# Two vectors of adaptive norm columns moved: from layer 0's MLP into its second phase and into the next projection

## The chip, the cores and the metric

The kernel runs on one core of a Trainium2 chip. The metric is device microseconds (us) of a launch, the median of several runs. The core has five engines with a queue each: PE (TensorE, matmuls), DVE (VectorE), ACT (ScalarE), POOL (GpSimd) and SP (SyncE, which here issues the DMA transfers). Each engine works off its own queue strictly in order; semaphores order the engines among each other.

## The reference

Two layers over 1024 tokens of width 1024, all in float32: layer 0 with sparse attention (NSA), layer 1 with sliding-window attention (SWA), each followed by a squared-ReLU MLP of width 4096. Every norm is modulated by a shift, a scale and a gate that come from one condition vector c:

```python
cond = jax.nn.silu(c)
for i in range(DEPTH):
    mod = cond @ ada_w[i] + ada_b[i]              # ada_w[i]: 1024 x 6144
    sh1, sc1, g1, sh2, sc2, g2 = jnp.split(mod, 6, axis=-1)
    h = modulate(rms_norm(x, norm_g[i, 0]), sh1, sc1)
    y = nsa_mixer(...) if i % 2 == 0 else swa_sink_mixer(...)
    x = x + (1 + g1)[:, None, :] * rms_norm(y, norm_g[i, 1])
    h = modulate(rms_norm(x, norm_g[i, 2]), sh2, sc2)
    y = squared_relu_mlp(h, mlp_w_up[i], mlp_w_down[i])
    x = x + (1 + g2)[:, None, :] * rms_norm(y, norm_g[i, 3])
```

So there are six vectors of 1024 to a layer, and each needs a matrix of 1024 x 1024 read once.

## The kernel before

**Stages.** In order of time: the NSA projection and attention, its output projection, layer 0's MLP (a first phase, up, 890 to 1228 us, and a second, down, 1228 to 1555), the SWA projection (about 1531 to 1672), SWA attention with its output projection, and layer 1's MLP (up to 2209, down to 2514). Tokens are eight tiles of 128 rows, t = 0 to 7; norm and turning go by halves of four tiles. Float32 products are made of three matmuls on a high and a low part of each operand (mm3, lines 572 to 574). Both MLP phases use Strassen-like sums of blocks: the first prepares sums of weights (ws, wt) on VectorE and GpSimd, and combines the products (u, sx); the second sums weights (wr) on GpSimd and splits them (st) on ScalarE and VectorE.

**A vector of the modulation ("ada").** `ada_steps` makes one vector of `mod`: eight loads of 128 x 1024 (`adaw`, 512 KB, L311, SP's queue), one L321 and seven L323 on VectorE that scale each by eight of the condition's numbers and add up into an accumulator (`ada`). With `single` a load is a step of its own; otherwise the first step issues three loads and each further step one, two steps ahead. Then `ada_cols` makes a column of it: two transposes (L344) and two reductions (L345, `adas`) on VectorE, four small matmuls (L349) on TensorE, and an addition (L350) on VectorE. `ada_pre(l, which)` makes the two vectors A and B (scale and shift) for a norm of layer l, that of the mixer (which = 0) or that of the MLP (which = 1); `ada_gate(l, which)` makes the gate vector behind it. A and B are used by the norm's last step, L496 on ScalarE, between the turning of the tiles on TensorE (L488, from `xr`) and the split in two parts (L498, L499).

**What sets the order.** There is no planner: the program lists steps (closures), and `spread` mixes two lists evenly. The `side` steps of a phase are mixed among its matmuls; `later(f, n)` puts f n steps behind. `chunks` runs the three parts of the SWA projection (the first four column blocks of q, called q0, then KV by tiles, then q1) and mixes each part with the next one's weight loads and with its share of a `side` list: with 16 side steps over 84 steps, six, six and four. `mlp_down` takes its side steps one to a main step and holds their finishes (the columns) until three quarters of its work are done; they then run one to a main step. Raw tiles for ada loads come from three buffers, and where a pool function is given (`self.slot`) from that pool of 40.

**Around the SWA projection.** Each tile of down's output is gated and added to x (L514, L522; x of before is loaded by L1799, and x of after stored by L1804), its root is taken (L450 on VectorE, L451 on GpSimd), and `xr` is scaled by L472. Four tiles are then turned. q's columns go through rope (L635 and L636 on VectorE, L637 and L639 on GpSimd, L638 on ScalarE) and out by DMA (qd); K's through L663, L666 and L667, V's through L689 and L690. Weights are split by L565 on ScalarE and L566 on VectorE. The first scores of SWA attention are L880 on TensorE, which reads qs from DRAM.

Of the kernel before, what the change touches and what calls it, by code (L numbers as in the profile page):

```python
# [30 lines left out]
LEAD_DOWN = 14  # L31
PAIRS0 = 6
TURN = (10, 20)
SIDE2 = 40
AHEAD = 3
DL = 4
DM = 9
# [7 lines left out]
QT = 5  # L45
# [37 lines left out]
def spread(a, b):  # L83

    out, n = [], 0
    for k, f in enumerate(b):
        while n < len(a) and n * len(b) <= k * len(a):
            out.append(a[n])
            n += 1
        out.append(f)  # L90
    return out + a[n:]


class Trunk:
# [924 lines left out]
    def nsa_unit(self, i, j):  # L1019
# [45 lines left out]
        def branch(b, K, c0, L, mask):  # L1065
# [6 lines left out]
            def head(g):  # L1072
                if g == 0:
                    u[b], nl["nm"], nl["l"] = [], m4("nm"), m4("l")
                if g % per == 0:
                    tiles.append(self.slot(name="p"))
                p, nm, l = tiles[-1][:, g % per * L:g % per * L + L], nl["nm"][:, g:g + 1], nl["l"][:, g:g + 1]
                u[b].append(p)
                s = [self.bank() for _ in range(nb)]
                for z in range(nb):  # L1080
                    self.scores(s[z][:, 0:N], u["q"], g, [v[:, c0 + z * w:c0 + z * w + N] for v in K()])

                def least():
                    for z in range(nb):
                        sl = slice(z * w, z * w + w)
                        self.masked(p[:, sl], s[z][:, 0:w], mask()[:, sl], nm, nm if z else 1e28)

                todo.append([least, lambda: self.exps(p, nm, l)])
                run(g)
# [6 lines left out]
            def weighed():  # L1096
                scale(u[b], nl["l"], b)

            return [(CH + L / 512, lambda g=g: head(g)) for g in range(4)] + [(0.0, lambda g=g: run(g)) for g in range(4, 5 + ML)] + [(0.3, weighed)]

        k0 = max(0, i - 4)
# [343 lines left out]
    def mlp_down(self, sd, w_down, side, post, last):  # L1445
# [101 lines left out]
        def go():  # L1547
            loaded, rest, more = 4, last, list(side)
            self.hold = held = []
            for n, steps in enumerate(main):  # L1550
                if n > 3 * n_q and held:
                    self.later(held.pop(0), 0)
                k = -(-len(more) // max(1, SIDE2 - n))
                steps = spread(more[:k], steps)
# [92 lines left out]
    def run(self):  # L1647
        nc, a = self.nc, self.a
# [31 lines left out]
        parts = self.nsa_project(hT, w_in)  # L1680
# [26 lines left out]
        side = self.ada_gate(0, 0) + self.ada_pre(0, 1)  # L1707
# [4 lines left out]
        for l in range(2):  # L1712
# [12 lines left out]
            take, up = self.up_setup(a["mlp_w_up"][l], lambda l=l: self.cols[l, 1])  # L1725
# [84 lines left out]

            if l == 0:
                parts = self.swa_project(hT2, a["swa_w_in"][0])
            side = self.ada_gate(0, 1, True) + self.ada_pre(1, 0, None, True) if l == 0 else self.ada_gate(1, 1, True)
            self.mlp(up, a["mlp_w_down"][l], side, self.ada_gate(1, 0) + self.ada_pre(1, 1) if l == 0 else [], post,
                     parts[0][0] if l == 0 else [])
            if l == 0:
                self.mark("swaproj")
                self.chunks(parts[:-1] + [(parts[-1][0], parts[-1][1][:4 * QT])])
                src = xd
            self.flush()  # L1820

# [27 lines left out]
```

## Time and profile before

| | us |
|---|---|
| median of 3 runs | 2529.06 (2527.83 to 2530.4) |
| profiled execution | 2529.18 |
| its span | 2527.4 |
| PE busy in the span | 2390.7 (95%) |
| DVE busy | 1924.7 (76%) |
| ACT busy | 1403.4 (56%) |
| POOL busy | 1323.6 (52%) |
| mean DMA rate | 173 GB/s |

The clock of TensorE was 0.979 of full speed on the mean. Busy shares are means over stages with different limits, so the views by stage and the waits of TensorE are of more use than the sums. An engine's idle time costs something only where TensorE comes to wait for it.

### The profile page before, as it was taken

How to read it: one execution, taken by the hardware profiler on the slowest of the kernel's cores; microseconds unless marked ns; L12 is line 12 of the kernel's file. 1: busy time of each engine (PE TensorE's matmuls, PEld its weight loads, DVE VectorE, ACT ScalarE, POOL GpSimd, SP SyncE). 2: the span in 40 equal slices, each digit the busy share in tenths (PEclk: the TensorE clock that was granted, in tenths of full speed). 3: DMA queues.
4: the chain of work that ended last, by engine and by line, in shares of the span. 5: the costliest groups of instructions: out<-in, count | busy, mean ns of one | idle time of the engine just before them, and what ended most of it. 6: DMA issues, size and time to landing. Idle time of an engine off the chain costs nothing.

```text
span 2527.4 us, 36711 instructions
## 1 busy us (share of the span) xinstructions
PE 2390.7 (95%) x11974; PEld 1988.7 (79%) x11974; DVE 1924.7 (76%) x3723; ACT 1403.4 (56%) x2959; POOL 1323.6 (52%) x1308
## 2 busy tenths in 40 slices
PE   6889999999999988999899999988999999999997
PEld 4779888888887767777788887867877688888886
DVE  7865579999895487777799768676768766687756
ACT  4532368898983473454435445377876354545433
POOL 4320566565662146555764622577744554694533
PEclk8999999999999999999999999999999999999999
DMA  7367723132226536556888654444323555597654
GB/s 281 100 216 238 249 80 97 39 93 62 78 68 150 141 117 200 188 199 201 316 327 321 239 186 173 142 140 111 84 86 120 183 176 183 193 319 243 224 186 171
DMA packets 239287, 437.14 MB, mean 173 GB/s; under 512 B 19236, under 2 KB 122872, under 8 KB 239096
## 3 DMA queue, kind: packets, MB, share of 16 engines
q1 hardware_dynamic: 210296, 405.44, 47.6%
q0 software_dynamic: 28800, 29.36, 4.9%
q8 instruction: 94, 1.54, 0.3%
q14 instruction: 97, 0.79, 0.1%
HBM read 320.42 MB, written 114.31 MB: 172 GB/s over the span
## 4 chain that ended last, share of the span: by engine, by line
PE 38%; DVE 5%; POOL 4%; issue 3%; DMA 3%; ACT 2%; SPq 0%; POOLq 0%; DVEq 0%; ACTq 0%
PE b L574 12%; PE b L572 12%; PE b L573 12%; POOL sx L1418 1%; DVE ada L323 1%; POOL qv L637 1%; ACT p L888 1%; PE o L925 1%; PE b L880 1%; DMA wr<-in_mlp_w_down_dram 1%; PE b L903 1%; DMA w<-in_mlp_w_up_dram 1%; DVE hl L1254 1%; DVE wt L1343 1%; DMA adaw<-in_ada_w_dram 0%
## 5 line engine op out<-in xcount | busy, mean ns | idle before, releaser
L572 PE MATMUL b<-hh,wt 128*128 128x512 f32 x896 | 355.5, 397 | 15.5 <-ACT wt L1342 15.3
L574 PE MATMUL b<-hh,wt 128*128 128x512 f32 x896 | 350.7, 395 | 8.7 <-DVE wt L1343 8.5
L573 PE MATMUL b<-st,st 128*128 128x512 f32 x896 | 349.8, 391 | 4.6 <-DVE st L1492 4.6
L573 PE MATMUL b<-hl,wt 128*128 128x512 f32 x896 | 352.2, 393 | 0.0
L574 PE MATMUL b<-st,st 128*128 128x512 f32 x896 | 348.9, 390 | 0.0
L572 PE MATMUL b<-st,st 128*128 128x512 f32 x896 | 330.8, 390 | 2.7 <-DVE u L1373 1.6
L888 ACT ACTIVATE p<-p,nm 128x256 f32<-128x256 f32 (+7 forms) x384 | 250.4, 656 | 46.9 <-DVE nm L884 45.5
L1031 POOL TENSOR_SCALAR p<-p,rl,nsam 128x640 f32<-128x640 f32 (+7 forms) x256 | 199.7, 793 | 136.3 <-DVE rl L1029 98.9
L1492 DVE TENSOR_TENSOR st<-wr,st 128x1024 fp32r<-128x1024 f32 (+1 forms) x128 | 189.8, 1482 | 55.8 <-ACT st L1491 36.5
L910 DVE TENSOR_TENSOR pT<-b,pT 128x512 fp32r<-128x512 f32 (+1 forms) x334 | 215.3, 657 | 21.7 <-ACT pT L909 21.3
L1491 ACT ACTIVATE st<-wr 128x1024 fp32r<-128x1024 f32 (+1 forms) x128 | 122.6, 958 | 195.1 <-POOL wr L1477 89.9
L1492 DVE TENSOR_TENSOR st<-sr,st 128x1024 fp32r<-128x1024 f32 (+1 forms) x128 | 200.8, 1569 | 32.6 <-ACT st L1491 30.4
L572 PEld LDWEIGHTS b<-hh,wt 128*128 128x128 f32 x896 | 170.7, 191 | 58.5 <-ACT wt L1342 24.6
L574 PEld LDWEIGHTS b<-hh,wt 128*128 128x128 f32 x896 | 170.2, 190 | 50.7 <-DVE wt L1343 15.2
L909 ACT ACTIVATE pT<-b 128x512 fp32r<-128x512 f32 (+1 forms) x334 | 185.5, 577 | 42.7 <-PE b L903 40.5
L925 PE MATMUL o<-pT,kv 128*128 128x512 f32 x484 | 194.7, 442 | 7.1 <-DVE pT L910 7.0
L573 PEld LDWEIGHTS b<-st,st 128*128 128x128 f32 x896 | 168.6, 188 | 41.5 <-DVE st L1492 6.8
L903 PE MATMUL b<-ident,p 128*128 128x128 f32 x1296 | 195.4, 274 | 4.7 <-POOL p L1629 2.5
L572 PEld LDWEIGHTS b<-st,st 128*128 128x128 f32 x896 | 168.5, 188 | 39.0 <-DVE u L1373 2.4
L1343 DVE TENSOR_TENSOR wt<-ws,wt 128x512 fp32r<-128x512 f32 x128 | 139.4, 1100 | 77.6 <-ACT wt L1342 76.8
L573 PEld LDWEIGHTS b<-hl,wt 128*128 128x128 f32 x896 | 170.4, 190 | 34.9
L574 PEld LDWEIGHTS b<-st,st 128*128 128x128 f32 x896 | 168.6, 188 | 34.7
(277 smaller groups left out, 6039.6 us busy)
## 6 DMA issues: line engine op xcount, KB each, us to landing
adaw<-in_ada_w_dram SPq DMA_DIRECT2D x96, 512.0 KB, 4.8
sr<-s SPq DMA_DIRECT2D x96, 512.0 KB, 4.5
wr<-in_mlp_w_down_dram SPq DMA_DIRECT2D x96, 512.0 KB, 6.6
w<-in_mlp_w_up_dram SPq DMA_DIRECT2D x76, 512.0 KB, 4.7
s<-sx SPq DMA_DIRECT2D x64, 512.0 KB, 4.2
x<-x SPq DMA_DIRECT2D x48, 512.0 KB, 3.2
s<-u SPq DMA_DIRECT2D x64, 256.0 KB, 2.2
we<-in_mlp_w_down_dram SPq DMA_DIRECT2D x64, 256.0 KB, 4.4
```

The costliest lines, as they stand in the source:

```text
L572: mm(out, s[0], m[0], start=first, stop=False)
L573: mm(out, s[0], m[1], start=False, stop=False)
L574: mm(out, s[1], m[0], start=False, stop=last)
L888: self.nc.scalar.activation(p, p, AF.Exp, scale=-1.0, bias=nm, accum_out=l)
L903: nc.tensor.transpose(pt[:, g * P:(g + 1) * P], p[:, cols], self.ident)
L909: nc.scalar.activation(x[:, 0, 0:w], pt[:, 0:w], AF.Copy)
L910: nc.vector.tensor_tensor(x[:, 1, 0:w], pt[:, 0:w], x[:, 0, 0:w].bitcast(F32), op=ALU.subtract)
L925: nc.tensor.matmul(out, s, m[:, z], start=n == 0 and z == 0, stop=n == len(tiles) - 1 and z == 1)
L1031: nc.gpsimd.tensor_scalar(ps[g], ps[g], rl[:, g:g + 1], gate[:, g, b:b + 1], op0=ALU.mult, op1=ALU.mult)
L1343: nc.vector.tensor_tensor(lo, r, hi.bitcast(F32), op=ALU.subtract)
L1491: nc.scalar.activation(hi, r, AF.Copy)
L1492: nc.vector.tensor_tensor(lo, r, hi.bitcast(F32), op=ALU.subtract)
```

## The change

Layer 0's MLP prepared, beside its own gate (0, 1), all that layer 1's mixer and MLP norms need: A and B of (1, 0) in the first phase, the gate (1, 0) and A and B of (1, 1) in the second. After the change the first phase makes only the gate (0, 1) (16 steps in place of 48), the second makes A and B of (1, 0) and then the gate (1, 0) (24 steps as before), and A and B of (1, 1) are a side list of the SWA projection (16 steps), with loads into the pool of 40. SIDE2, which sets how many side steps go to a main step of down, goes from 40 to 46.

```diff
-SIDE2 = 40
+SIDE2 = 46
...
             if l == 0:
                 parts = self.swa_project(hT2, a["swa_w_in"][0])
-            side = self.ada_gate(0, 1, True) + self.ada_pre(1, 0, None, True) if l == 0 else self.ada_gate(1, 1, True)
-            self.mlp(up, a["mlp_w_down"][l], side, self.ada_gate(1, 0) + self.ada_pre(1, 1) if l == 0 else [], post,
+            side = self.ada_gate(0, 1, True) if l == 0 else self.ada_gate(1, 1, True)
+            self.mlp(up, a["mlp_w_down"][l], side, self.ada_pre(1, 0) + self.ada_gate(1, 0) if l == 0 else [], post,
                      parts[0][0] if l == 0 else [])
             if l == 0:
                 self.mark("swaproj")
-                self.chunks(parts[:-1] + [(parts[-1][0], parts[-1][1][:4 * QT])])
+                self.chunks(parts[:-1] + [(parts[-1][0], parts[-1][1][:4 * QT])], self.ada_pre(1, 1, self.slot))
                 src = xd
             self.flush()
```

Three places in the order of instructions. First, VectorE in layer 0's up phase, around the second ada step of the vector (ws and wt are weight sums, u are products). Before:

```order
L1373 TENSOR_TENSOR u_11328<-b_11329,u_10838 128x512
L323 SCALAR_TENSOR_TENSOR ada_11238<-adaw_11535,cond,ada_11238 128x1024
L1373 TENSOR_TENSOR u_10838<-b_11354,u_11328 128x512
L1343 TENSOR_TENSOR wt_11351<-w_11219,wt_11351 128x512
L1373 TENSOR_TENSOR u_11328<-b_11377,u_10838 128x512
L1373 TENSOR_TENSOR u_11328<-b_11377,u_11328 128x512
```

After:

```order
L1343 TENSOR_TENSOR wt_11432<-ws_11430,wt_11432 128x512
L323 SCALAR_TENSOR_TENSOR ada_11318<-adaw_11684,cond,ada_11318 128x1024
L1373 TENSOR_TENSOR u_11443<-b_11444,u_10887 128x512
L1373 TENSOR_TENSOR u_10887<-b_11469,u_11443 128x512
L1343 TENSOR_TENSOR wt_11466<-w_11337,wt_11466 128x512
L1325 TENSOR_TENSOR ws_11483<-w_11455,w_11457 128x512
```

Layer 1's up phase reads, before and after:

```order
L1343 TENSOR_TENSOR wt_20590<-ws_20588,wt_20590 128x512
L323 SCALAR_TENSOR_TENSOR ada_20476<-adaw_20842,cond,ada_20476 128x1024
L1373 TENSOR_TENSOR u_20601<-b_20602,u_20045 128x512
L1373 TENSOR_TENSOR u_20045<-b_20627,u_20601 128x512
L1343 TENSOR_TENSOR wt_20624<-w_20495,wt_20624 128x512
L1325 TENSOR_TENSOR ws_20641<-w_20613,w_20615 128x512
```

The rows of layer 0 after are those of layer 1, line by line.

Second, SP's queue at the end of down, where the tiles 4 to 7 of x are stored (x_4 to x_7 at L1804) and x of tile 7 is loaded (from x_0_7, L1799). Before:

```order
L1804 DMA x_4_10618<-x_15929 128x1024
L1804 DMA x_5_10619<-x_15960 128x1024
L1799 DMA x_16041<-x_0_7_2934 128x1024
L624 DMA rope_16055<-rope_368 128x1024
L547 DMA w_16534<-in_swa_w_in_dram 128x2x512
L1804 DMA x_6_10620<-x_16005 128x1024
L1804 DMA x_7_10621<-x_16041 128x1024
```

After:

```order
L1804 DMA x_4_10618<-x_15850 128x1024
L1804 DMA x_5_10619<-x_15881 128x1024
L311 DMA adaw_15959<-in_ada_w_dram 128x1024
L311 DMA adaw_15961<-in_ada_w_dram 128x1024
L311 DMA adaw_15963<-in_ada_w_dram 128x1024
L1804 DMA x_6_10620<-x_15926 128x1024
L1799 DMA x_15966<-x_0_7_2934 128x1024
L624 DMA rope_15993<-rope_368 128x1024
L547 DMA w_16482<-in_swa_w_in_dram 128x2x512
L1804 DMA x_7_10621<-x_15966 128x1024
```

Three ada loads and the store of tile 6 now stand ahead of the load of tile 7's x.

Third, VectorE in the KV part, from the rope of K in tile 1 on. Before:

```order
L663 TENSOR_TENSOR kn_16526<-b_16501,cos 128x128
L666 TENSOR_TENSOR rope_16527<-b_16501,sin_190 128x2x32 x2
L690 TENSOR_TENSOR V_16491<-b_16461,V_16491 128x2x64
L566 TENSOR_TENSOR wl_16537<-w_16534,wh_16536 128x4x4x64
L690 TENSOR_TENSOR V_16491<-b_16501,V_16491 128x2x64
L663 TENSOR_TENSOR kn_16565<-b_16540,cos 128x128
```

After:

```order
L663 TENSOR_TENSOR kn_16474<-b_16448,cos 128x128
L666 TENSOR_TENSOR rope_16475<-b_16448,sin_190 128x2x32 x2
L344 STREAM_TRANSPOSE adat_16489<-ada_15958 128x512
L690 TENSOR_TENSOR V_16438<-b_16408,V_16438 128x2x64
L344 STREAM_TRANSPOSE adat_16492<-ada_15958 128x512
L345 TENSOR_REDUCE adas_16488<-adat_16489 128x16
L566 TENSOR_TENSOR wl_16485<-w_16482,wh_16484 128x4x4x64
L690 TENSOR_TENSOR V_16438<-b_16448,V_16438 128x2x64
L345 TENSOR_REDUCE adas_16488<-adat_16492 128x16
```

and TensorE at the same place, where tile 1's last matmuls (into b_16448) and tile 2's first (into b_16502) stand:

```order
L573 MATMUL b_16448<-wl_16250,hh_15773 128x256
L574 MATMUL b_16448<-wh_16249,hl_15774 128x256
L349 MATMUL b_16495<-adas_16488,fold 32x8 x4
L572 MATMUL b_16502<-wh_15982,hh_15701 128x256
L573 MATMUL b_16502<-wl_15983,hh_15701 128x256
```

The column chain of A (1, 1) stands between: VectorE has its second reduction behind an L566, and TensorE has the four L349 that read it ahead of tile 2.

## Rows read from the trace of the kernel before

**Rows 1.** The page, part 1: busy time, share and instructions of each engine.

```profile
PE 2390.7 (95%) x11974; PEld 1988.7 (79%) x11974; DVE 1924.7 (76%) x3723; ACT 1403.4 (56%) x2959; POOL 1323.6 (52%) x1308
```

**Rows 2.** The page, part 4: the chain that ended last, its shares by line.

```profile
PE b L574 12%; PE b L572 12%; PE b L573 12%; POOL sx L1418 1%; DVE ada L323 1%; POOL qv L637 1%; ACT p L888 1%; PE o L925 1%; PE b L880 1%; DMA wr<-in_mlp_w_down_dram 1%; PE b L903 1%; DMA w<-in_mlp_w_up_dram 1%; DVE hl L1254 1%; DVE wt L1343 1%; DMA adaw<-in_ada_w_dram 0%
```

**Rows 3.** Busy us by stretch: length, PE, PEld, DVE, ACT, POOL, PEclk, DMA, GB/s.

```profile
945.60:1228.52 282.92, 270.39 (x1174) 217.70 (x1173) 212.66 (x266) 129.10 (x217) 157.36 (x106) 0.98 0.59 202
1936.20:2209.47 273.27, 267.83 (x1170) 217.54 (x1170) 191.01 (x243) 132.58 (x220) 155.13 (x109) 0.99 0.51 178
1228.52:1325.74 97.22, 89.84 (x380) 71.64 (x379) 91.05 (x53) 36.91 (x42) 77.96 (x37) 0.98 0.91 336
2209.47:2294.67 85.20, 85.20 (x377) 70.57 (x376) 66.20 (x33) 36.06 (x42) 76.54 (x38) 1.00 0.90 313
1570.00:1640.00 70.00, 67.54 (x395) 59.02 (x394) 46.33 (x89) 28.30 (x46) 36.74 (x32) 0.98 0.44 139
1640.00:1720.00 80.00, 65.34 (x343) 54.14 (x342) 56.19 (x181) 53.73 (x162) 63.98 (x87) 0.91 0.56 154
```

**Rows 4.** Waits of PE in layer 0's up phase: us, times, longest.

```profile
PE b L574 <- DVE wt L1343: 6.2, 4, 2.9
...
PE b L349 <- DVE adas L345: 1.7, 2, 1.1
```

**Rows 5.** The same in layer 1's up phase.

```profile
PE b L574 <- DVE wt L1343: 0.4, 1, 0.4
```

**Rows 6.** Timeline of PE after the turn: start, us, [idle before, releaser].

```profile
1245.37 0.50 PE L573 MATMUL b<-st,st 128*128 128x512 f32 x1 [2.31 <-DVE st L1492]
```

**Rows 7.** Timeline of POOL at the turns to down, layers 0 and 1.

```profile
1224.12 1.29 POOL L1476 TENSOR_TENSOR wr<-wr,we 128x512 f32<-128x512 f32 x1 [3.17 <-PE b L574]
...
2198.90 1.29 POOL L1476 TENSOR_TENSOR wr<-wr,we 128x512 f32<-128x512 f32 x1 [0.59 <-PE b L574]
```

**Rows 8.** L323 in layer 0's down: duration ns min/median/max, starts.

```profile
L323 DVE SCALAR_TENSOR_TENSOR ada<-adaw,cond,ada x21: 1272/2202/2325, 1237.0 to 1361.9; 128x1024 f32<-128x1024 f32 x21
```

**Rows 9.** Timeline of DVE, a column chain in layer 0's up phase.

```profile
1205.12 1.30 DVE L344 STREAM_TRANSPOSE adat<-ada 128x512 f32<-128x512 f32 x2
...
1208.11 0.68 DVE L345 TENSOR_REDUCE adas<-adat 128x16 f32<-128x512 f32 x1
```

**Rows 10.** Timeline of SP's queue at the end of down.

```profile
1561.52 0.38 SPq L1799 DMA_DIRECT2D x<-x  x1
...
1566.26 2.34 SPq L1804 DMA_DIRECT2D x<-x  x2
```

**Rows 11.** The page, part 6: loads of ada, KB each, us to landing.

```profile
adaw<-in_ada_w_dram SPq DMA_DIRECT2D x96, 512.0 KB, 4.8
```

**Rows 12.** Timeline of PE at the turning of tiles 4 to 7.

```profile
1573.93 0.88 PE L488 MATMUL b<-ident,xr 128*128 128x128 f32 x6 [0.80 <-DVE xr L472]
1576.37 1.32 PE L488 MATMUL b<-ident,xr 128*128 128x128 f32 x8 [1.57 <-ACT h L496]
```

**Rows 13.** Timeline of DVE at the same place.

```profile
1571.44 2.43 DVE L472 TENSOR_SCALAR xr<-x,r 128x1024 f32<-128x1024 f32 x2 [0.56 <-POOL r L451]
```

**Rows 14.** Timeline of DVE in the KV part.

```profile
1607.32 0.29 DVE L663 TENSOR_TENSOR kn<-b,cos 128x128 f32<-128x128 f32 x1 [2.34 <-POOL kn L667]
...
1609.70 2.09 DVE L566 TENSOR_TENSOR wl<-w,wh 128x1024 fp32r<-128x1024 f32 x1 [1.62 <-ACT wh L565]
```

**Rows 15.** Timeline of PE in the KV part.

```profile
1607.05 0.28 PE L572 MATMUL b<-wh,hh 128*128 128x256 f32 x1
```

**Rows 16.** All L349 of the kernel: idle of PE before them, times.

```profile
  DVE adas L345: 4.2, 4
```

**Rows 17.** Timeline of DVE at the start of SWA attention.

```profile
1653.02 0.69 DVE L635 TENSOR_TENSOR qv<-b,rope 128x512 f32<-128x512 f32 x1 [3.61 <-POOL qv L637]
```

**Rows 18.** Waits of PE from 1640 to 1720.

```profile
PE b L880 <- DMA qs<-qd: 6.6, 4, 3.3
```

**Rows 19.** Waits of DVE in layer 0's up phase.

```profile
DVE ada L323 <- DMA adaw<-in_ada_w_dram: 12.8, 10, 2.0
```

## The prediction

> **What bounds the kernel now.** I read the page first. TensorE is busy 95% of the span, VectorE 76%, ScalarE and GpSimd about half [rows 1], and the chain that ended last runs for 36% over three matmul lines [rows 2]. So a change off TensorE is worth only the time for which TensorE stands still, or runs at the lower of its clock levels after it stood still. Second I read the stages apart: of the up phase, the span from the eighth addition of a product (L1373) to the first matmul of down, of down its first group (to the first L1510), once for layer 0 and once for layer 1, then the SWA projection [rows 3]. The columns to look at are the length, PE busy and the clock. Third I read the waits of TensorE by stage, and last the timelines at the places that the change touches.
>
> The profiled execution took 2529.18 us (span 2527.4), the median of the three runs is 2529.06; the sum is made against the first, and the difference of 0.12 plays no part.
>
> **What the trace offers.** Layer 1's up phase carries one ada vector beside its matmuls, layer 0's three; the products, weights and combinations are the same. After the change layer 0 carries one as well, and VectorE's queue of that phase then reads like that of layer 1. So layer 1 of the same execution is a model of what layer 0 becomes.
>
> **A. Up phase of layer 0: minus 9.6.** Two vectors leave it: 16 loads of 512 KB on SP's queue, 2 L321, 14 L323 and the column work of each (two transposes, two reductions, four L349, L350). At 1.27 us at least for an L323 [rows 8] and 2.5 for the column work of a vector [rows 9] that is some 23 us of VectorE. What it is worth on TensorE is the difference of the two stretches: 282.92 less 273.27, that is 9.65 [rows 3]. It is made of idle time (282.92 less 270.39 is 12.5, against 5.4) and of the clock (0.98 against 0.99). The waits say where: for the low halves of the weights from VectorE (wt, L1343) 6.2 us in layer 0 and 0.4 in layer 1, for L349's own input 1.7 and none [rows 4, 5]. I take 9.6, with 6 to 11 as ends: the upper is 7.1 of idle time and one and a half hundredths of clock, the lower is the idle time of these two waits less what layer 1 keeps of them (6.2 + 1.7 - 0.4 = 7.5), less 1.5 for new alignments.
>
> **B. First group of down: minus 5, between 0 and 9.** It lasts 97.22 us in layer 0 and 85.20 in layer 1, with no idle time there, against 7.4 and a clock of 0.98 here [rows 3]; idle time plus two hundredths of 97 is 9.3. Its stalls lie at the turn of the phases, as in the 2.31 us for st (L1492) [rows 6]. Behind them is work that up left over: GpSimd's first sum of down's weights starts 4.4 us before down's first matmul (1228.52) in layer 0, 10.6 before (2209.47) in layer 1 [rows 7]. Fewer vectors in up let this work end in time. But down keeps 24 ada steps, eight to a vector: they were gate (1, 0) and the two vectors of pre (1, 1), and are the two of pre (1, 0) and gate (1, 0). SIDE2 changes nothing: 24 over 46, rounded up, is one step to a main step, as 24 over 40 was. Of those steps 21 are L323, and here they take 2.20 us in the median [rows 8]. Between no return and all of 9.3 I take 5. That down finishes a pre where it finished a gate costs nothing: the finishes stay held until down's end, and the columns are wanted only by the first L496 of the norm, behind VectorE work of several us. If that cover were gone, it would be one column chain of two transposes and two reductions, 2.5 us [rows 9].
>
> **C. Projection, first quarter (q0): plus 5, between 2 and 8.** Sixteen steps of pre (1, 1) now run here, 6 of them in q0. On SP's queue the first three loads and the store of tile 6 come ahead of the load of x for tile 7. That load was issued at 1561.52, the store of tile 6 at 1566.26 [rows 10]: it is 4.7 us later, for the store waits until x of tile 6 is added. On VectorE an L321 stands in front that waits for the first load (4.8 us to landing [rows 11]), with all of L514, L566 and both L472 of tiles 5 and 6 queued behind it, and two L323 stand ahead of tile 7's L522. TensorE has no cover left at this place: it already waits 0.80 for xr of tiles 6 and 7 and 1.57 for h [rows 12], with xr written from 1571.44 [rows 13]. So the delay of 4.7 goes through, and I take 5. The ends are one load's delay less the old wait of 2.4, and the same with two long L323 on top.
>
> The L323 stretch from 1.27 to 2.20 us where GpSimd is busy beside them [rows 8]. The Trainium skill (SBUF — State Buffer, Who interferes with whom) says that a VectorE instruction with two inputs in SBUF and a GpSimd instruction that reads SBUF exclude each other for a whole instruction; by that rule the two roots on GpSimd for tiles 6 and 7 could each stand behind an L323, an estimate of 2 x 1.27 = 2.5 more, and the total would be 2531. The trace agrees as far as the L323 go, and does not show what the roots would wait.
>
> **D. Projection, KV part, first column chain: plus 7, between 2 and 9.** The finish of pre (1, 1)'s first vector puts four L349 into TensorE's queue right behind the 24 matmuls of KV tile 1; tile 2 stands behind them. L349 needs the second reduction, and VectorE's queue has before it: L663 and L666 of tile 1, two transposes, L690, a reduction, L566, L690. By the times of before: tile 1's L663 starts at 1607.32 and the three rope steps end at 1607.8; two transposes 1.3, L690 0.2, a reduction 0.7 give 1610.0; L566 in its turned form takes 2.09 [rows 9, 14], then L690 and the reduction: 1613.0. TensorE starts tile 2 at 1607.05 in before [rows 15], so it would stand for 5.6 to 5.9 us, since engines start the next instruction a little before the end that the trace gives for the last. The window 1570 to 1640 shows what such a stall of 2.5 us costs in clock, two hundredths of 70 [rows 3], 1.4. Together 7. The waits of L349 that the trace has are shorter, 4.2 us over 4 [rows 16], and give the lower end: 1.05 each and its clock.
>
> **E. Second chain, at the start of attention: plus 1.5, between 0 and 4.** Its L349 stand ahead of the first 32 L880. Of its four VectorE steps two lie in the 3.61 us for which VectorE waits there [rows 17]; two of 0.6 come after it at 1653.0, and TensorE gets there about 2 us earlier. Attention then waits 6.6 us for qs by DMA anyway [rows 18], which can swallow it.
>
> **F. Order of the first half's transposes: plus 0.5, between 0 and 2.** All 32 L488 of tiles 0 to 3 now stand in a row, where they alternated with 24 matmuls of down; ScalarE's L496 can fall behind them. The upper end is about one such wait as the second half has, 1.57 [rows 12].
>
> The sum: -9.6 - 5 + 5 + 7 + 1.5 + 0.5 = -0.6, so 2528.5 us. The changes cancel: what comes out of the MLP comes back in a projection in which VectorE has time (46 of 70 us) but TensorE's queue stands behind it.
>
> **The rivals.** *Faster, the projection absorbs it.* VectorE is idle for a third of the projection [rows 3], loads can land early, L349 can be reached late because C has already delayed TensorE. Then A 9.6 and B 7 stand against C 3 and D 3 and nothing else: 2518.5. Against it stands the strict order of the queues, in which idle time elsewhere does not help.
>
> *Slower, the column chain decides.* TensorE's queue stands at L349 behind a reduction, and VectorE's behind an L566 that waits for ScalarE. If the two chains cost 8 and 4, C 6 and F 1, while B gives nothing back, because its 24 steps are what clogs down, the sum is -9.6 + 19 = +9.4: 2538.5. It decides from the point where the stalls of the projection pass 20 us against a gain of 14.6. For it speaks that ada steps stay in down; against it that L349 waited 1.05 in the mean of those four cases [rows 16].
>
> *Slower, up gives little.* The three vectors in up may only fill time in which VectorE waits: it waits 12.8 us there for ada loads alone [rows 19], and those waits would turn into others. Then A is 1.7 (L349's own wait) and B 4, and the sum is +8: 2537. Against it stands layer 1, which shows the phase with one vector.
>
> **How the numbers follow.** What a measurement here can tell from no change is 0.2%, or 5 us. The forecast (cancelling within 5 us) gets 0.38, the faster rival with its neighbours 0.35, the column chain 0.15, the small gain in up 0.12. So faster 0.35, same 0.38, slower 0.27. The range to leave out 2 in 10 reaches past both rivals' centres a little: 2516 to 2540; the forecast's own is 2523.5 to 2533.5.
>
> **What would show it.** A: the up stretch of layer 0 near 273 us, and its wait for VectorE's wt near 0.4. B: the first group of down near 92, with GpSimd's first sum some 10 us ahead. C: an idle stretch of TensorE before L488 on xr or x of tile 7 of 5 to 7 us in place of 0.8. D: one wait of L349 for adas of about 5.6 in the KV part. E: one of about 2 ahead of L880. The forecast is wrong if the stretch from down's last group to attention's first L880 grows by less than 6 or more than 20 us, or the up stretch shrinks by less than 6.

## The result: slower by 14 us

The changed kernel took 2542.53 us in the median of four runs (2538.55 to 2544.04), the kernel before, run beside it, 2528.44: a ratio of 1.0055, with a 95% interval of 1.0042 to 1.0068. The forecast was 2528.5, with a range of 2516 to 2540, so the time lies 2.5 us past its end. The rival that a stalled column chain decides (2538.5) comes nearest in time, but it is not what happened: the largest cost stands at another place.

The page of the changed kernel, part 1 (busy time, share, instructions):

```profile
PE 2395.0 (94%) x11974; PEld 1996.1 (79%) x11974; DVE 1924.7 (76%) x3723; ACT 1406.6 (55%) x2959; POOL 1314.0 (52%) x1308
```

TensorE runs as many matmuls as in [rows 1] and stands still for longer. Where is told by the stretches. Busy time by stretch of the changed kernel, columns as in [rows 3]: the up phase, the first group of down, then three stretches of the projection (from the first transposition of tiles 4 to 7, L488, to VectorE's first L663, on to its last, and on to attention's first L880):

```profile
947.31:1221.69 274.38, 268.02 (x1164) 218.02 (x1163) 191.28 (x242) 131.93 (x219) 154.37 (x108) 0.99 0.52 182
1221.69:1315.02 93.33, 87.67 (x380) 70.74 (x379) 87.68 (x50) 35.89 (x41) 68.60 (x35) 1.00 0.92 337
1555.91:1609.89 53.98, 39.90 (x180) 33.01 (x179) 39.87 (x56) 17.07 (x26) 23.30 (x18) 0.81 0.61 216
1609.89:1638.41 28.52, 23.11 (x182) 22.84 (x181) 20.16 (x48) 9.92 (x18) 6.85 (x10) 0.88 0.62 221
1638.41:1668.50 30.09, 27.84 (x132) 22.61 (x131) 20.16 (x31) 7.52 (x15) 13.46 (x14) 1.00 0.52 149
```

and the last three of the kernel before:

```profile
1565.35:1604.43 39.08, 36.68 (x180) 30.26 (x179) 28.30 (x42) 14.98 (x21) 25.10 (x18) 0.96 0.48 174
1604.43:1625.70 21.27, 21.21 (x175) 20.91 (x174) 13.06 (x37) 9.91 (x18) 8.63 (x10) 1.00 0.35 124
1625.70:1652.76 27.06, 27.06 (x122) 22.31 (x121) 12.11 (x23) 6.97 (x14) 13.07 (x13) 1.00 0.53 141
```

In the first of the three the same 180 matmuls take 53.98 us in place of 39.08. TensorE idles 14.1 us there, it idled 2.4, and its granted clock is 0.81 in place of 0.96. Single executions scatter: the part ahead of layer 0's MLP, whose instructions nothing here changed except in one experiment, lets the up phase's stretch begin between 942.3 and 950.3 us in the other profiles. So stages are compared by their lengths, and the kernel before was run twice more for its profile:

| stretch (us) | before, three executions | changed | difference | forecast |
|---|---|---|---|---|
| up phase (from the ninth addition L1373, which the prediction calls the eighth, 945.60 in before) | 282.7 to 283.2 | 274.4 | -8.6 | A -9.6 |
| first group of down | 95.5 to 97.3 | 93.4 | -3.0 | B -5 |
| rest of down, first half's transposes, to the first L488 of tiles 4 to 7 | 239.5 | 240.8 | +1.3 | F +0.5 |
| on to VectorE's first L663 (q0) | 38.5 to 39.1 | 54.0 | +15.1 | C +5 |
| on to the last L663 (KV) | 21.3 | 28.5 | +7.2 | D +7 |
| on to the first L880 | 27.1 | 30.1 | +3.0 | E +1.5 |
| on to the same addition in layer 1 (1936.20 in before) | 282.4 to 283.4 | 281.7 | -1.2 | 0 |

The sum is +13.8, against 14.1 by the medians. Five of six steps stand within their bounds; C is three times its value and nearly twice its upper bound. Differences are against the mean of the three executions. Over all profiles, those of the experiments below with them, the up phase takes 273.5 to 276.7 us in the twelve kernels with one vector there and 280.8 to 283.2 in the four executions with three, so A's gain is about 7 on the mean.

The waits of TensorE, up phase of layer 0 in the changed kernel:

```profile
PE b L572 <- ACT wt L1342: 5.8, 5, 2.5
PE b L574 <- DVE wt L1343: 0.4, 1, 0.4
```

Of what [rows 4] showed, 0.4 of the 6.2 us for VectorE's wt is left and the wait of L349 is gone, as in [rows 5]; the wait for ScalarE's half of wt, 4.5 us before, has grown to 5.8. GpSimd's first sum for down comes 8.9 us ahead of down (1221.69), in place of 4.4 [rows 7]:

```profile
1212.81 1.30 POOL L1476 TENSOR_TENSOR wr<-wr,we 128x512 f32<-128x512 f32 x1 [2.01 <-PE b L574]
```

But the wait that B named, TensorE's for st (L1492), did not go with it. The waits in down's first group, before:

```profile
PE b L573 <- DVE st L1492: 4.6, 5, 2.3
PE b L572 <- DVE u L1373: 1.6, 1, 1.6
PE b L572 <- ACT st L1491: 1.2, 1, 1.2
```

and changed:

```profile
PE b L573 <- DVE st L1492: 4.5, 5, 1.7
PE b L572 <- ACT st L1491: 1.2, 1, 1.2
```

What went is the wait of 1.6 us for u, and the granted clock was 1.00 in place of 0.98.

The waits of TensorE from 1520 to 1680, changed:

```profile
PE b L349 <- DVE adas L345: 7.7, 2, 5.4
PE b L488 <- DVE xr L472: 7.2, 2, 6.8
PE b L488 <- DVE qv L635: 4.0, 1, 4.0
PE b L488 <- ACT h L496: 2.9, 1, 2.9
```

L349's two waits are D and E, 5.4 and 2.3; all such waits of the kernel before came to 4.2 over four [rows 16]. Those of L488 are C; in [rows 12] they were 0.8 and 1.6. The timeline of TensorE there:

```profile
1563.43 2.40 PE L488 MATMUL b<-ident,xr 128*128 128x128 f32 x10 [6.82 <-DVE xr L472]
1569.83 1.54 PE L488 MATMUL b<-ident,xr 128*128 128x128 f32 x6 [4.00 <-DVE qv L635]
1571.71 1.75 PE L488 MATMUL b<-ident,xr 128*128 128x128 f32 x7 [0.34 <-DVE xr L472]
1576.39 1.11 PE L488 MATMUL b<-ident,xr 128*128 128x128 f32 x4 [2.93 <-ACT h L496]
```

TensorE begins with tile 4 at 1555.91, 9.4 us earlier than before (1565.35), and stands still from 1556.6 on. It has nothing else to do there, for the order of its queue has changed. Counted from the queue (q: matmuls of the projection on tiles 0 to 3, of which 24 make a product):

| | q | L488 | q | L488 | q |
|---|---|---|---|---|---|
| before | 42 | 4 | 24 | 28 | 96 |
| changed | 36 | 32 (in a row) | | | 120 |

Twenty-four matmuls, 5.4 us at 0.227 each, stood between the first four transposes and the other 28, and now stand behind all of them. The cause is in the program: `later(f, n)` counts steps, and `chunks` hands the ada steps to `go` as steps of their own. Each of them makes the norm's waiting work come due one step sooner, measured in matmuls.

### The profile page after: what moved, and what is told of

Its sections match the earlier page's. It is cut to its first block, busy times and chain, and to the rows that moved or that the text cites. A ratio compares the mean times of both kernels' runs of the same rounds, so it can differ in the third digit from the quotient of the medians.

```text
span 2541.4 us, 36728 instructions
## 1 busy us (share of the span) xinstructions
PE 2395.0 (94%) x11974; PEld 1996.1 (79%) x11974; DVE 1924.7 (76%) x3723; ACT 1406.6 (55%) x2959; POOL 1314.0 (52%) x1308
## 4 chain that ended last, share of the span: by engine, by line
PE 66%; DVE 13%; DMA 7%; issue 5%; ACT 4%; POOL 4%; SPq 1%; POOLq 0%; DVEq 0%; ACTq 0%
PE b L572 16%; PE b L574 16%; PE b L573 16%; PE b L880 5%; PE o L925 5%; PE b L903 4%; DMA w<-in_mlp_w_up_dram 2%; DVE p L884 1%; DMA o<-o 1%; DVE ada L323 1%; DVE pT L910 1%; DMA adaw<-in_ada_w_dram 1%; DVE hl L1254 1%; POOL sx L1418 1%; DVE wt L1343 1%
## 5 line engine op out<-in xcount | busy, mean ns | idle before, releaser
L888 ACT ACTIVATE p<-p,nm 128x256 f32<-128x256 f32 (+7 forms) x384 | 250.4, 656 | 47.6 <-DVE nm L884 46.2
L1031 POOL TENSOR_SCALAR p<-p,rl,nsam 128x640 f32<-128x640 f32 (+7 forms) x256 | 200.7, 796 | 137.0 <-DVE rl L1029 95.5
L1492 DVE TENSOR_TENSOR st<-wr,st 128x1024 fp32r<-128x1024 f32 (+1 forms) x128 | 191.7, 1497 | 49.5 <-ACT st L1491 31.2
L1492 DVE TENSOR_TENSOR st<-sr,st 128x1024 fp32r<-128x1024 f32 (+1 forms) x128 | 202.1, 1579 | 34.4 <-ACT st L1491 32.1
L909 ACT ACTIVATE pT<-b 128x512 fp32r<-128x512 f32 (+1 forms) x334 | 185.8, 577 | 39.1 <-PE b L903 36.8
```

The costliest lines, as they stand in the source:

```text
L888: self.nc.scalar.activation(p, p, AF.Exp, scale=-1.0, bias=nm, accum_out=l)
L909: nc.scalar.activation(x[:, 0, 0:w], pt[:, 0:w], AF.Copy)
L1031: nc.gpsimd.tensor_scalar(ps[g], ps[g], rl[:, g:g + 1], gate[:, g, b:b + 1], op0=ALU.mult, op1=ALU.mult)
L1492: nc.vector.tensor_tensor(lo, r, hi.bitcast(F32), op=ALU.subtract)
```

## The experiments

Theory 1: steps are counted, so side steps pull the transposes ahead of their cover, and the columns' L349 block TensorE's queue. Theory 2, the rival: the ada steps' own work (VectorE, loads) is the cost, wherever it is put. Ratios are against runs of the kernel before on the same chip. Not all runs were on one chip, so what a kernel loses is compared by its own difference from the kernel before: 14.1 us for the change.

**Empty steps.** The kernel before, with

```diff
-self.chunks(parts[:-1] + [(parts[-1][0], parts[-1][1][:4 * QT])])
+self.chunks(parts[:-1] + [(parts[-1][0], parts[-1][1][:4 * QT])], [lambda: None] * 16)
```

> The kernel before, with 16 empty steps mixed into the projection as the change mixes its 16 ada steps; no instruction is added. Theory 1 (steps are counted): the norm's late work is put behind by a number of steps, so empty steps bring 28 of the second half's 32 transposes ahead of 24 matmuls of q that covered them; TensorE waits for the norm some 5 us more than the 2.4 of before, and the kernel is slower by 3 to 6 us, about 2533. Theory 2 (the ada steps' own work, loads and VectorE time, is the cost): nothing changes, within 1 us of before, and the waits at L488 stay at 2.4.

Measured: 2532.05, ratio 1.0022 (1.0011 to 1.0032), 4.5 us slower with not one instruction more. TensorE's queue reads q 42, L488 32, q 120, and q0 takes 43.76 us, 4.9 more than the 38.9 of before, of which 2.2 are idle time (4.6 in place of 2.4) and the rest goes with the lower granted clock, 0.88 in place of 0.96:

```profile
1565.23:1608.99 43.76, 39.13 (x180) 32.06 (x179) 28.60 (x41) 14.99 (x21) 21.00 (x18) 0.88 0.41 144
```

The waits of L488 in it:

```profile
PE b L488 <- DVE qv L635: 3.0, 1, 3.0
PE b L488 <- DVE xr L472: 0.9, 1, 0.9
PE b L488 <- ACT h L496: 0.7, 1, 0.7
```

A transposition does not read what L635 writes; L635 reads q's product. So TensorE has run ahead of the rope and, as far as the operands tell, lacks a free bank. Theory 1 is shown for this part.

**Steps not counted.** The changed kernel, each side step joined with the step behind it:

```diff
-            self.go(spread(side[:k], steps))
+            mixed = spread([(f, 0) for f in side[:k]], [(f, 1) for f in steps])
+            joined, held = [], []
+            for f, own in mixed:
+                held.append(f)
+                if own:
+                    joined.append(lambda fs=tuple(held): [g() for g in fs])
+                    held = []
+            self.go(joined + held)
```

> The changed kernel, with each ada step of the projection run inside the next step, so that it isn't counted. Theory 1: the 24 matmuls of q stand ahead of 28 transposes again; TensorE's idle time at L488 falls from 14 us to 6 to 9 (the late load of x and the L323 stay), L349 stands one KV tile later and waits 2 to 5; about 2535, 5 to 9 faster than the changed kernel. Theory 2: the same ada work at the same place, 2541 to 2543.

Measured: 2547.47 (1.0083, 1.0068 to 1.0098), a miss: `chunks` serves the NSA projection too, and there the edit cost some 9 us ahead of the first MLP (the up phase's stretch begins at 956.4, in the changed kernel at 947.3). So it was repeated for the SWA projection alone:

> The changed kernel, with each ada step of the SWA projection alone run inside the next step, so that it isn't counted; the run before this one did the same in the NSA projection too, where it cost some 10 us before the first MLP. Theory 1: from the up phase on that run lost 4 us less than the changed kernel, so 2537 to 2539; TensorE's idle time at L488 is 9 to 10 us in place of 14. Theory 2: 2541 to 2544.

Measured: 2535.73 (1.0033, 1.0020 to 1.0046), 7.9 us over the kernel before in place of 14.1, a little better than theory 1 had it. The order is that of before again (4, 24, 28, 96). q0 takes 50.85 us, but with 27 matmuls of KV more in it, since VectorE comes late to L663; at 0.12 us each that is 3.2 us, and what is comparable is some 47.6:

```profile
1556.59:1607.44 50.85, 41.62 (x207) 34.84 (x206) 40.45 (x56) 16.45 (x25) 23.57 (x17) 0.87 0.64 224
```

The order is worth 54.0 - 47.6 = 6.4 us here in q0, and 4.9 with empty steps. Of q0's 15.1 us it leaves some 9 to 10. But 2.1 of the 6.4 are lost again behind q0: from KV's first matmul to attention's first L880 this kernel takes 63.9 us, the changed one 61.7.

**L349 later.** The changed kernel, with the four matmuls of the projection's columns as a step of their own:

```diff
-        pt = self.bank()
-        for z in range(4):
-            nc.tensor.matmul(pt[32 * z:32 * z + 32, 0:8], self.fold, part[:, z::4], ...)
-        nc.vector.tensor_tensor(dst, pt[:, 0:8], self.adab[...], op=ALU.add)
+        def fold():
+            ...
+        self.later(fold, 8)      # for (1, 1) alone
```

> The changed kernel, with the four L349 of the projection's two vectors put eight steps behind their reductions (for the first vector two KV tiles, 5.8 us of matmuls, later; the second stays at the start of attention, where the list is flushed). Theory 1: the 5.4 us wait of L349 in the KV part goes, and about 2.5 us of lower clock behind it; 7 to 8 faster than the changed kernel, 2535. Theory 2: VectorE's work is the same and only the place of the wait moves, 2540 to 2543.

Measured: 2534.44 (1.0029, 1.0015 to 1.0044), 6.9 us over the kernel before in place of 14.1. KV takes 21.42 us, as in the kernel before:

```profile
1607.88:1629.30 21.42, 21.42 (x184) 21.14 (x183) 18.26 (x43) 8.38 (x13) 10.93 (x10) 1.00 0.84 292
```

VectorE does 18.26 us of work there, 5 more than in the kernel before, and it costs nothing. Step D is shown: the place of L349 is the whole cost of the KV part. In the changed kernel VectorE has the second reduction behind L566, as [rows 14] led to expect:

```profile
1614.66 0.64 DVE L345 TENSOR_REDUCE adas<-adat 128x16 f32<-128x512 f32 x1
1615.23 2.01 DVE L566 TENSOR_TENSOR wl<-w,wh 128x1024 fp32r<-128x1024 f32 x1
1617.11 0.33 DVE L690 TENSOR_TENSOR V<-b,V 128x128 fp32r<-128x128 f32 x1
1617.31 0.72 DVE L345 TENSOR_REDUCE adas<-adat 128x16 f32<-128x512 f32 x1
```

and L349 starts right behind it on TensorE:

```profile
1618.08 0.30 PE L349 MATMUL b<-adas,fold 128*32 128x8 f32 x8 [5.41 <-DVE adas L345]
```

**Both edits.**

> Both edits at once: ada steps not counted, and the projection's L349 eight steps behind their reductions. Theory 1: the two costs lie at different places and add up, 8 less by L349 and 4 less by the order: 2529 to 2532. If they hide the same wait: 2533 to 2536.

Measured: 2536.59 (1.0035, 1.0022 to 1.0048). They do not add up, and the time is 0.6 past even the second expectation. KV still takes 24.0 us, since VectorE enters it late and L349 waits 4.7 even eight steps behind. Against the run with L349 later alone, the order saves 4.6 us up to KV's first matmul (44.6 against 49.3), and from there to attention's first L880 5.3 are lost (60.7 against 55.4). So the price of the order is one in q0; with L349 out of the way the projection as a whole gains nothing by it.

**No ada steps in q0.** `chunks(..., start=1)`:

> The changed kernel, with the 16 ada steps spread over KV and q1 alone (none in q0, so SP's queue and VectorE are free of them while tiles 4 to 7 are normed, and 24 matmuls of q stand ahead of 28 transposes as in the kernel before). Theory 1 (counted steps, and ada work in the norm's tail): the cost in q0 falls from 14 us to what the run with 40 steps in down showed, 6 at most; L349 still stands in the KV part in front of a tile and waits 2 to 6; 2529 to 2534. Theory 2 (ada work costs anywhere in the projection): 2540 or more.

Measured: 2539.11 (1.0047, 1.0030 to 1.0064), a miss. q0 falls to 45.8, again with 27 matmuls of KV in it. Up to KV's first matmul it is 39.4, against 50.9 in the changed kernel and 35.7 before: without ada steps 11.5 of C's 15.1 us are gone. But 16 steps in KV and q1 cost there: KV takes 32.7 us, with TensorE waiting 5.18 for GpSimd's kn (L667) and 3.92 at L349:

```profile
1609.79 0.48 PE L676 MATMUL b<-ident,kn 128*128 128x128 f32 x1 [5.18 <-POOL kn L667]
...
1623.24 0.29 PE L349 MATMUL b<-adas,fold 128*32 128x8 f32 x8 [3.92 <-DVE adas L345]
```

With L349 eight steps later as well:

> Ada steps in KV and q1 alone, and L349 eight steps behind the reductions. Theory 1: nothing of the projection's costs is left but the norm's own wait, as in the run with 40 steps in down: 2522 to 2527, faster than the kernel before by 1 to 5. Theory 2: ada work in KV and q1 costs on, 2535 or more.

Measured: 2534.14 (1.0029, 1.0017 to 1.0040), a miss too. KV falls to 23.1, and the second vector's L349 waits 5.4 at attention's start. So theory 2 holds in part: these steps find no free place in the projection.

**Which part of the ada work.** Three runs take apart what is left of C. First, x of tile 7 is loaded with that of tile 6, ahead of the ada loads:

```diff
+                for v in (t, 7) if t == 6 and l == 0 else (t,):
+                    if v not in xs:
+                        xs[v] = self.slot(name="x")
+                        nc.sync.dma_start(xs[v], x1[v])
```

> The changed kernel, with x of tile 7 loaded together with x of tile 6, ahead of the ada loads and of the stores, as on SP's queue neither before nor after. Theory a (the late load, the step of the prediction): TensorE's idle time at L488 falls by about 4 of 14 us, and the kernel to 2537 to 2539. Theory b (VectorE's queue: the three ada steps ahead of tile 7's norm, and the 24 matmuls in the wrong place): nothing changes, 2541 to 2544, since tile 7's L522 had no idle time before it in the changed kernel's trace.

Measured: 2540.77 (1.0054, 1.0040 to 1.0069), 12.8 us over the kernel before, and so the changed kernel again within the interval; q0 takes 52.3. Second, the loads without VectorE's work:

```diff
+            if (l, m) == (1, 4) and k < 6:
+                return
```

> The changed kernel, with the first six ada steps of the projection (those in q0) issuing their loads but not their VectorE instructions, so the first vector is the sum of two parts of eight (six parts are left out). Theory b: the 3.4 us of L321 and L323 and the 1.0 us of waiting for the first load that stand on VectorE ahead of tile 7's norm go, the order of the transposes stays: 2537 to 2539. Theory a: the loads and the place of x of tile 7 on SP's queue stay about the same, so 2541 to 2544.

Measured: 2539.29 (1.0052, 1.0037 to 1.0066), 11.3 us over, between the two theories; q0 50.9. VectorE reaches tile 7's L524 (L522 in the other kernels) sooner, and now x is missing there:

```profile
1563.36 1.28 DVE L524 SCALAR_TENSOR_TENSOR x<-yg,r,x 128x1024 f32<-128x1024 f32 x1 [1.42 <-DMA x<-x]
```

That load was issued at 1555.73 behind three ada loads and took over 7 us. Third, VectorE's work without the loads:

```diff
+            if (l, m) == (1, 4) and k < 6:
+                u[k] = self.one      # the gate's row, resident
```

> The changed kernel, with the first six ada steps of the projection reading the gate's row, which is resident, in place of loads (so the first vector is not the one of the reference); all six now come ahead of tile 7's xr on VectorE, 7.1 us in place of 3.4 and a wait of 1.0. Theory b: TensorE waits 2 to 3 us longer at L488 than in the changed kernel: 2543 to 2546. Theory a: without loads the store of tile 6 and the load of x for tile 7 stand as before, 2536 to 2539.

Measured: 2544.33 (1.0067, 1.0054 to 1.0079), 16.4 us over, as theory b had it; q0 53.4, with TensorE waiting 11.4 us for xr. Loads alone and VectorE's work alone each keep most of the loss, and the order of the queue, which is the changed kernel's in all three runs, stays with both. How the rest of C splits between loads and VectorE is not shown.

**No ada steps in the projection.** The two vectors as last of 40 side steps in down, and no side list in the projection:

```diff
-self.ada_pre(1, 0) + self.ada_gate(1, 0) if l == 0 else []
+self.ada_pre(1, 0) + self.ada_gate(1, 0) + self.ada_pre(1, 1) if l == 0 else []
```

> The changed kernel, with the two vectors of pre (1, 1) as last 16 of 40 side steps in down, none in the projection. Theory 1: the gain in up and in down's first group (8.5 and 3.9 us in the changed kernel's trace) stays and all costs in the projection go, except 0 to 2 us at the norm's first half: 2516 to 2520, faster than both. Theory 2: ada work costs where VectorE and the DMA are already full, and down is fuller than the projection (VectorE 90% busy in its first group): 2527 or more.

Measured: 2523.62 (0.9983, 0.9971 to 0.9995), 3.9 us faster than the kernel before (the interval is 1 to 7) and so some 18 faster than the changed one; a smaller gain than theory 1 had it, a larger one than theory 2. And the two vectors left out altogether:

> The changed kernel without pre (1, 1): the projection has no side steps, and layer 1's MLP norm uses the columns of its mixer norm (the two vectors are left out). It shows what the moves out of the up phase are worth by themselves. Theory 1 (the gain of 12 us in up and down arrives early at a norm whose own chain sets the time, and 4 to 7 of it are swallowed in q0): the start of KV is 4 to 6 us earlier than in the kernel before, and the total 2521 to 2524. Rival (the gain is whole, and what was missing in the run with 40 steps in down was the price of 16 more steps there): KV 10 us earlier, 2515 to 2518.

Measured: 2526.07 (0.9994, 0.9984 to 1.0004). q0 takes 41.45 us, 2.6 more than before, though no ada step is in it:

```profile
1558.28:1599.73 41.45, 36.91 (x180) 30.83 (x179) 30.84 (x48) 16.95 (x26) 26.21 (x18) 0.92 0.51 180
```

TensorE comes early to a norm that is not done, and waits 4.5 us for its xr:

```profile
PE b L488 <- DVE xr L472: 4.5, 2, 2.3
```

So 2.6 us of the gain are swallowed there. But the two totals fit no full account. The stages of this one execution add up to some 7 less than those of before, the times to 0.8 less by the medians (by the interval, 4.0 less to 1.0 more); the profiled execution was 2.4 below its own median. What the move out of up is worth alone stays open, between nothing and 7 us.

**The kernel before again**, unchanged and with SIDE2 = 46:

> The kernel before, unchanged: a second execution of it, against which the stages of the changed kernels can be laid. If the first execution was an ordinary one, the stretch from the eighth addition of a product to down's first matmul is again 10 us longer than in layer 1 and the first group of down 10 to 12 longer, each within 2 us; if the first was long there by chance, both are shorter by 4 or more, and the gain of 12 us in the MLP is smaller than the one pair of executions shows.

> The kernel before with SIDE2 = 46. It gives the same one side step to a main step, so the same order of instructions: 2525 to 2531, and a third execution of the stages of before. If SIDE2 mattered, down's stretches would differ by over 2 us.

Measured: 2527.69 (1.0005, 0.9993 to 1.0016) and 2526.86 (1.0000, 0.9988 to 1.0011). SIDE2 does nothing: every engine has the same instructions in the same order. The up phase takes 282.7 and 283.2 us, down's first group 96.3 and 95.5: the gains of A and B are no accident of one execution, and the first execution had 1.0 to 1.8 us more to lose in B than these two.

## Why the prediction was wrong, step by step

**A (-9.6)** was right in mechanism and a little large: -8.6. Layer 1 was a good model of the up phase: 274.4 us against its 273.3. **B (-5)** measured -3.0, within its bounds, but partly by luck: the waits for st that it named stayed (4.6 and 4.5 us), although GpSimd's first sum came earlier as forecast. **D (+7) and E (+1.5)** were right: 7.2 and 3.0, with the wait of 5.41 where 5.6 to 5.9 were worked out, and L349's second wait 2.25. **F (+0.5)** measured 1.3, of which 0.5 is the wait for ScalarE's h that it named.

**C (+5, between 2 and 8) is the step that failed**, at 15.1. It laid the loads' delay of 4.7 us on TensorE as it stood in the kernel before, with 2.4 us of idle time in front of it. Three things were wrong in that. The runs price each by itself; as the prices come from different kernels, their sum is an estimate:

- TensorE's order. The prediction saw for the first half that all 32 L488 stand in a row (F), and took the second half's order as unchanged. It wrote that TensorE has no cover left at this place; it had 24 matmuls of q, 5.4 us, and the counted steps took them away. Empty steps alone cost 4.9 us in q0, and counting undone gives back 6.4.
- The gain's end. The 12 us won in the MLP were entered in the sum whole, but they bring TensorE to the norm of tiles 4 to 7 early, where y, x, root and xr follow each other. With no ada step there 2.6 us are lost in q0.
- What is left, 15.1 less 2.6 less 4.9 to 6.4, is 6 to 8 us, the part that C was about. It is a little more than forecast, but not by the mechanism named. The late load of x is no cause by itself: with it early q0 keeps 52.3 of 54.0. VectorE's queue comes to tile 7 later than the load does. The changed kernel's rows:

```profile
1559.62 0.75 DVE L321 TENSOR_SCALAR ada<-adaw,cond 128x1024 f32<-128x1024 f32 x1 [1.02 <-DMA adaw<-in_ada_w_dram]
1560.29 1.28 DVE L514 TENSOR_TENSOR yg<-y,gbc 128x512 f32<-128x512 f32 x2
1561.50 1.22 DVE L566 TENSOR_TENSOR wl<-w,wh 128x1024 fp32r<-128x1024 f32 x1
1562.63 1.41 DVE L472 TENSOR_SCALAR xr<-x,r 128x1024 f32<-128x1024 f32 x2
1563.96 2.60 DVE L323 SCALAR_TENSOR_TENSOR ada<-adaw,cond,ada 128x1024 f32<-128x1024 f32 x2
1566.47 1.28 DVE L522 SCALAR_TENSOR_TENSOR x<-yg,r,x 128x1024 f32<-128x1024 f32 x1
...
1570.90 0.75 DVE L472 TENSOR_SCALAR xr<-x,r 128x1024 f32<-128x1024 f32 x1 [0.53 <-POOL r L451]
```

TensorE's 6.82 us end with the xr of tiles 5 and 6, written from 1562.6 on. The first ada step takes 1.7 us of them (1.02 of waiting, and the L321); the rest is VectorE's other work and waits of the norm, which no matmul covers any more. L522 of tile 7 has no idle time in front of it, so x had landed. The SP rows bear the prediction's order out. In the changed kernel x of tile 7 (L1799) is issued 3.4 us after the end of the first two stores:

```profile
1551.66 2.59 SPq L1804 DMA_DIRECT2D x<-x  x2
1554.35 1.71 SPq L311 DMA_DIRECT2D adaw<-in_ada_w_dram  x3
1557.20 0.33 SPq L1804 DMA_DIRECT2D x<-x  x1
1557.62 0.45 SPq L1799 DMA_DIRECT2D x<-x  x1
```

and in the kernel before 0.1 after it, at 1561.52 [rows 10]:

```profile
1556.44 4.99 SPq L1804 DMA_DIRECT2D x<-x  x2
```

That is 3.3 us of delay, where 4.7 were forecast.

With the other steps as measured and C at its forecast value the sum would be +3.7 us, within the 0.2% of the forecast: the excess of C alone made the change a clear loss.

On the rule of the Trainium skill (SBUF — State Buffer, Who interferes with whom) nothing was decided. In the changed kernel no root (L451) of these tiles stood beside an L323: GpSimd's last root ahead of tile 7 ends at 1559.3, the two L323 run from 1563.96 to 1566.56, and tile 7's root starts at 1570.32 and takes 0.55 us. So the 2.5 us that the rule would have added are not there.

## What to carry to other kernels

Where work is queued by a count of steps, even a step that issues nothing moves all that waits: compare the whole order of the bound engine, not the place where the change was made. A gain far upstream is worth its full size only if the next stage's own chain has slack; ask what TensorE meets when it arrives 10 us early. And in a strictly ordered queue the price of four tiny matmuls is set by what their input stands behind.

## What was not expected of the hardware

Taking away one of several causes changed little (12.8 us of loss with x early, 11.3 without VectorE's steps in q0, against 14.1): behind the first another was waiting, as the 1.42 us for x showed. A load of 512 KB behind three others of that size was over 7 us on its way, against a median of 3.3 for loads of x. And after TensorE had idled 14.1 of 54 us its granted clock was 0.81 in that stretch, and the same 180 matmuls were busy for 39.90 us in place of 36.68: some 3 us on top of the idle time.
